# Four moves in a hybrid attention encoder: the rotary exchange on ScalarE, later scores, the first x tiles of chunk two, and w_out's casts behind V's copy

## The chip, the cores and the metric

The kernel runs on one core of a Trainium2 chip. A core has TensorE (matmuls, with a separate load of the weights), VectorE, ScalarE, GpSimd, and SyncE, which here issues nearly all DMAs. The metric is the time of one execution on the device in microseconds (us); less is better.

## The reference

One layer of an encoder with two groups of attention heads, applied to a prompt of 1024 tokens and to a sample of 256 tokens, each with 16 learned meta tokens in front. All is float32.

```python
u = rms_norm(h, norm_w) @ w_in                     # 2048 -> 6656
qa, ka, va, za, qb, kb, vb, zb = split(u)          # 8 q, 2 k, 2 v, 8 gate heads of 128; then 4 x 8 heads
qa, ka = rope(rms_norm(qa)), rope(rms_norm(ka))
ya = softmax(qa @ ka.T / sqrt(128)) @ va * silu(za)          # 8 global heads, 4 to one k and v
qb, kb = rms_norm(qb), rms_norm(kb)
yb = softmax(window(qb @ kb.T) / sqrt(128) + bias) @ vb * silu(zb)   # window of 8 x 16, and the meta tokens
y = h + concat(ya, yb) @ w_out                     # 2048 -> 2048
```

The rotary embedding (rope) acts on the two halves of a head's 128 features apart, one for the row and one for the column: in each half, `_rotate` takes x1*c - x2*s and x1*s + x2*c of two quarters x1 and x2 of 32 features.

## The kernel before

A float32 product is made of three matmuls of fp32r: each operand is split into a high part, a cast on ScalarE (L65), and a low part, a subtraction on VectorE (L66). `split` records both; hi*hi, hi*lo and lo*hi are L219 to L221 in the projection, L368 to L370 in the scores, L409 to L411 in the values and L1038 to L1040 in the output projection. TensorE gets its tiles through this pair, and the names say which: wh and wl for w_in, x for the activations, ph and pl for probabilities, q for queries, yh and yl for the attention's output, wm for w_out.

The tokens are projected in two chunks. Chunk one holds 512 tokens (16 meta, 256 sample, 240 prompt), with the features on the 128 partitions. Chunk two holds the other 784 tokens of the prompt, as a block of 512 and one of 272. A strip is 128 output columns of w_in, one head of q, k, v or the gate z, over 16 tiles of 128 input features. There are 52 strips per chunk, for some of which w_in is read from a copy in DRAM in the second chunk. The result of a strip lies in a bank of PSUM (pool pp) and is evacuated by a function of its kind:

- `qk_evac` (L249) squares it on ScalarE (ms, L252), sums over partitions on GpSimd (m2, L254), and for a rotary strip also copies it times the norm's gain to t (L258), makes ts, in which neighbouring groups of 32 partitions are exchanged, by four DMAs (L261), and forms t*c + ts*s on VectorE (L263 to L265; L263 and L264 in place). `rsqrt` (L72 to L77) gives the factor of the norm, and L268 the finished q or k. Rotary strips are the 8 q and 2 k strips of the global heads: 10 evacuations in chunk one, 20 in chunk two (512 and 272).
- `v_rows` (L278) scales v by the token's norm on VectorE into vt (L280), which TensorE transposes; in chunk two `rows_out` (L521) copies the transposed rows on ScalarE from a bank of the pool tp to vl (L533, and L538 for a last piece of fewer than 128 rows) and stores them. The first product of the output projection takes that same bank, so it waits for these copies.
- `z_evac` (L290) makes the gate.

Attention is generators that are put between strips. `run_due` (L234) is called at places, two per strip; `put(n, f)` (L246) sets a part to run n places on. In chunk one `later` (L710) puts the scores and softmax of a head at the first number of `PARTS`, its values at the second, after the place at which its q strip was made. A softmax takes its maximum over partitions on GpSimd (ma, L319), subtracts it on VectorE (L388), applies the exponential and casts ph on ScalarE, and sums on GpSimd (tot, L337), with VectorE's L346 behind. The last sample head of chunk one runs its attention (`attend_sample`, L415: Sm at L425, S at L429) while chunk two begins. The x tiles of chunk two are loaded, multiplied by the norm's gain and split by `load_all_x` (L148): L162 on ScalarE, L163 on VectorE, for a 512 and a 272 piece of each of 16 tiles kt.

The output projection (`outproj`, L1077) uses seven products in the manner of Strassen; `w_operand` (L1015) splits a tile of w_out (ww into wm) and `y_operand` (L980) one of the attention's output (yl into yh and yl). Its first 16 casts of w_out and its first two of y stand where chunk two's last strips and the last local head end.

A scheduler orders the instructions of each engine from a simulated timeline and the dependencies; a dependency without a semaphore (`NoSync`) can be added by hand to set the order of two instructions on one engine.

Of the kernel before, what the change touches and what calls it, by code (L numbers as in the profile page):

```python
# [25 lines left out]
M3 = 3 * NMETA  # L26
# [18 lines left out]
WTYPE = (0, 1, 1, 2)  # L45
FILL = 1
LATE = 48
PARTS = 2, 6
WCH = 4
LAG = 6  # L50
TH = (NP + NS) // 2
# [1 line left out]
FB = 512  # L53
FH = DM // 2
QA, KA, VA, ZA, QB_, KB, VB, ZB = 0, 8, 10, 12, 20, 28, 36, 44
AGAIN = {KA, VA, ZA} | {a + h for a in (QB_, KB, VB, ZB) for h in range(4, 8)}


class Kern:
# [3 lines left out]
    def split(self, hi, lo, full):  # L63
        nc = self.nc
        self.hi = nc.scalar.copy(hi, full).ins  # L65
        return nc.vector.tensor_tensor(out=lo, in0=full, in1=hi.bitcast(F32), op=ALU.subtract).ins  # L66

    def rsqrt(self, ms, n):

# [78 lines left out]
    def load_all_x(self):  # L148


        nc, self.xload = self.nc, {}
        for kt in range(KT):
            w = self.nw[:, kt:kt + 1]
            self.xs[kt] = []
            ta = self.x.tile([P, 2, NB], F32R, tag="xa", name="x", align_bytes=ALIGN)
            tb = self.xb.tile([P, NX], F32R, tag="xb", name="xb", align_bytes=ALIGN)
            o = 0
            for h, l in ((ta[:, 0], ta[:, 1]), (tb[:, :NT2], tb[:, NX - NT2:])):
                r, n = l.bitcast(F32), l.shape[1]
                with self.tc.issue_after(self.early):  # L160
                    self.xload.setdefault(kt, nc.sync.dma_start(r, self.x2d[kt][:, o:o + n]).ins)
                nc.scalar.activation(h, r, AF.Copy, scale=w)  # L162
                nc.vector.scalar_tensor_tensor(out=l, in0=r, scalar=w, in1=h.bitcast(F32), op0=ALU.mult, op1=ALU.subtract)  # L163
                self.xs[kt].append((h, l))
                o += n
        self.tc.add_manual_dep(self.qstore, self.xload[KT // 2].name, mybir.DependencyInfo(
            mybir.DependencyClass.NoSync, mybir.DependencyReason.DATA), reason="x first")
        self.behind = [None] + [self.xload[c] for c in range(WCH - 1, KT, WCH)]
        for d, c in self.consts:
            with self.tc.issue_after(self.xload[KT - 1]):  # L170
                nc.sync.dma_start(d, c)
# [77 lines left out]
    def qk_evac(self, ps, o, n, wc, rope, segs, full=None):  # L249
        nc = self.nc  # L250
        ms = self.ev.tile([P, n], F32, tag="ev", name="ms")
        nc.scalar.activation(ms[:], ps[:, :n], AF.Square, scale=P ** -0.5)  # L252
        m2 = self.ev.tile([P, n], F32, tag="ev", name="m2")
        nc.gpsimd.partition_all_reduce(m2[:], ms[:], P, RED.add)  # L254
        nc.vector.tensor_tensor(out=m2[:], in0=m2[:], in1=self.eb[:, o:o + n], op=ALU.add)
        if rope is not None:
            t = self.ev.tile([P, n], F32, tag="ev", name="t")
            nc.scalar.activation(t[:], ps[:, :n], AF.Copy, scale=wc)  # L258
            ts = self.ev.tile([P, n], F32, tag="ev", name="ts")
            for i in range(4):  # L260
                nc.sync.dma_start(ts[32 * i:32 * i + 32], t[32 * (i ^ 1):32 * (i ^ 1) + 32])  # L261
            c, s = rope
            nc.vector.tensor_tensor(out=t[:], in0=t[:], in1=c, op=ALU.mult)  # L263
            nc.vector.tensor_tensor(out=ts[:], in0=ts[:], in1=s, op=ALU.mult)  # L264
            nc.vector.tensor_tensor(out=t[:], in0=t[:], in1=ts[:], op=ALU.add)  # L265
        r = self.rsqrt(m2[:], n)
        if rope is not None:
            nc.vector.tensor_tensor(out=r[:], in0=t[:], in1=r[:], op=ALU.mult)  # L268
        else:
            d = r[:] if full is None else full  # L270
            nc.vector.scalar_tensor_tensor(out=d, in0=ps[:, :n], scalar=wc, in1=r[:], op0=ALU.mult, op1=ALU.mult)
        for a, m, hi, lo in segs:
            if lo is None:
                nc.sync.dma_start(hi, r[:, a:a + m])
            else:
                self.split(hi, lo, r[:, a:a + m])

    def v_rows(self, ps, o, n):  # L278
        vt = self.ev.tile([P, n], F32, tag="ev", name="vt")
        self.nc.vector.tensor_tensor(out=vt[:], in0=ps[:, :n], in1=self.rb[:, o:o + n], op=ALU.mult)  # L280
        return vt

    def v_turn(self, vt, offs, m=P):
# [131 lines left out]
    def attend_sample(self, q, zs, k, km, vals, vmeta, tab, ydst):  # L415

        nc = self.nc
        ps = self.sp.tile([P, 2, QB], F32, tag="sp", name="sp")
        ps = ps[:].rearrange("p a b -> p (a b)")
        for i in range(2):  # L420
            nc.tensor.matmul(ps[:, HALF * i:HALF * i + HALF], k[:, P * i:P * i + P], q[:, 64 * i:64 * i + HALF], start=True, stop=True)
        pm = self.sp.tile([P, 2, QB], F32, tag="sp", name="sm_ps")
        nc.tensor.matmul(pm[:M3, 0, :], km, q, start=True, stop=True)
        sm = self.sm.tile([M3, QB], F32, tag="Sm", name="Sm")
        nc.scalar.activation(sm[:], pm[:M3, 0, :], AF.Copy, scale=SCALE)  # L425
        s = self.s.tile([P, 2, QB], F32, tag="S", name="S")
        s = s[:].rearrange("p a b -> p (a b)")
        w = 2 * HALF
        nc.vector.scalar_tensor_tensor(out=s[:, :w], in0=ps[:, :w], scalar=SCALE, in1=tab, op0=ALU.mult, op1=ALU.add)  # L429

        def ap(t, off, dims):
            return bass.AP(t.tensor, t.offset + off, [list(t.ap[0])] + dims)

        def gather(name, op):

            m = self.t.tile([P, QB], F32, tag="t", name=name)
            nc.vector.tensor_copy(ap(m[:], 0, [[192, 2], [1, 64]]), ap(s, 0, [[320, 2], [1, 64]]))
            nc.vector.tensor_tensor(out=m[:, 64:192], in0=s[:, 64:192], in1=s[:, 192:320], op=op)
            return m

        ma = self.all_max(gather("m1", ALU.max), sm)
        v = ap(s, 0, [[HALF, 2], [1, HALF]])
        nc.vector.tensor_tensor(out=v, in0=v, in1=ap(ma[:], 0, [[64, 2], [1, HALF]]), op=ALU.subtract)
        nc.scalar.activation(s[:, :w], s[:, :w], AF.Exp)
        pm3 = self.meta_probs(sm, ma, 1.0)
        tot = self.all_sum(gather("a1", ALU.add), sm)
        yield
        po = self.op.tile([P, QB], F32, tag="po", name="po")
        nc.tensor.matmul(po[:], vmeta, pm3[:], start=True, stop=False)
        for i in range(2):  # L450
            nc.tensor.matmul(po[:, 64 * i:64 * i + HALF], vals[:, i, :], s[:, HALF * i:HALF * i + HALF], start=False, stop=i == 1)
        self.put_y(po, tot, zs, ydst)
# [68 lines left out]
    def rows_out(self, vt, n, dst, o):  # L521

        nc = self.nc
        for a in range(0, n, 4 * P):
            offs = range(a, min(n, a + 4 * P), P)
            full = [x for x in offs if x + P <= n]
            t = self.ev.tile([P, 4, P], F32, tag="ev", name="vl")
            tp = self.tp.tile([P, 4, P], F32, tag="tp", name="tp")
            for i, x in enumerate(offs):
                m = min(P, n - x)  # L530
                self.turn_ins(nc.tensor.transpose(tp[:m, i, :], vt[:, x:x + m], self.ident[:]).ins)
            f = len(full)
            nc.scalar.copy(t[:, :f, :], tp[:, :f, :])  # L533
            nc.sync.dma_start(dst[o + a:o + a + P * f].rearrange("(t p) d -> p t d", p=P), t[:, :f, :])
            if f < len(offs):
                m = n - offs[f]
                t = self.ev.tile([m, P], F32, tag="ev", name="vl")
                nc.scalar.copy(t[:], tp[:m, f, :])  # L538
                nc.sync.dma_start(dst[o + n - m:o + n], t[:])
# [67 lines left out]
    def chunk1(self):  # L607
# [2 lines left out]
        self.due, self.late, self.turn, self.behind, self.turned, self.tie = iter(()), [], False, [], [], (1, 0)  # L610
        self.woff, self.second, self.projected, self.sums = 0, False, 0, self.w_sums()
        self.scale2 = [self.one2.tile([P, T2], F32, tag=n, name=n) for n in ("rb2", "eb2")]
        self.xsq = {}
        self.start_chunk(T1)
        vm3s = self.vm3s
        self.vm3s = vm3s + [self.v.tile([P, P], F32R, tag="vmz", name="vm3")]
# [363 lines left out]
    def y_operand(self, p, t, r):  # L980
        nc = self.nc
        if p in (1, 2):
            his, los, full = [], r, [l[:].bitcast(F32) for l in r]
            for l, f in zip(los, full):
                his.append(self.w.tile([P, WCH, P], F32R, tag="wh", name="yh"))
                self.split(his[-1][:], l[:], f)
            return his, los
        if p == 4:
            v = r[0]
# [24 lines left out]

    def w_operand(self, r):  # L1015
        w = self.x.tile([P, 2, FB], F32R, tag="xa", name="wm", align_bytes=ALIGN)
        self.split(w[:, 0, :], w[:, 1, :], r)
        return w

    def x_load(self, p, t, b):  # L1020

# [292 lines left out]
```

## Time and profile before

| | |
|---|---|
| median of 3 runs | 2173.13 us (2171.66 to 2174.37) |
| profiled execution | 2170.17 us |
| its span, first to last instruction | 2168.4 us |
| TensorE busy | 2154.2 us, 99% of the span |
| VectorE, ScalarE, GpSimd busy | 76%, 51%, 24% |
| TensorE's share of the chain that ended last | 92% |
| granted clock of TensorE | 1.000 |

The profile is one execution. A busy row gives an engine's busy time, its share of the span and its number of instructions. A row of the timeline gives the start in us, the duration in us, the engine, the line, the operation, the tiles written and read, their shape and how many alike stand in the row, and in brackets how long the engine had stood idle and what ended that. A row of waits gives the engine, the tile and line that waited, what it waited for, and then the total in us, the number of times and the longest. SPq is the queue in which SyncE issues DMAs. Durations of neighbouring instructions of an engine overlap at their ends.

### The profile page before, as it was taken

How to read it: one execution, taken by the hardware profiler on the slowest of the kernel's cores; microseconds unless marked ns; L12 is line 12 of the kernel's file. 1: busy time of each engine (PE TensorE's matmuls, PEld its weight loads, DVE VectorE, ACT ScalarE, POOL GpSimd, SP SyncE). 2: the span in 40 equal slices, each digit the busy share in tenths (PEclk: the TensorE clock that was granted, in tenths of full speed). 3: DMA queues.
4: the chain of work that ended last, by engine and by line, in shares of the span. 5: the costliest groups of instructions: out<-in, count | busy, mean ns of one | idle time of the engine just before them, and what ended most of it. 6: DMA issues, size and time to landing. Idle time of an engine off the chain costs nothing.

```text
span 2168.4 us, 34088 instructions
## 1 busy us (share of the span) xinstructions
PE 2154.2 (99%) x11745; PEld 1877.5 (87%) x11745; DVE 1644.9 (76%) x2989; ACT 1115.1 (51%) x2291; POOL 522.7 (24%) x250
## 2 busy tenths in 40 slices
PE   9999999999999999999999999999999999999999
PEld 7888878888888999989999999999999988888887
DVE  7787886777874899896798998677787877545763
ACT  6565554555554666665666666444443454232230
POOL 1232331221311234332133324324333312000000
PEclk9999999999999999999999999999999999999999
DMA  8667789988664333334333344654443364662663
GB/s 301 220 206 224 235 301 308 325 286 278 214 195 144 100 115 107 113 114 132 106 110 106 105 124 145 192 162 131 132 133 122 115 201 152 238 226 99 233 223 107
DMA packets 263182, 383.83 MB, mean 177 GB/s; under 512 B 44992, under 2 KB 112992, under 8 KB 263008
## 3 DMA queue, kind: packets, MB, share of 16 engines
q1 hardware_dynamic: 263008, 381.65, 54.1%
q8 instruction: 92, 1.51, 0.3%
q14 instruction: 82, 0.67, 0.1%
HBM read 281.01 MB, written 100.38 MB: 176 GB/s over the span
## 4 chain that ended last, share of the span: by engine, by line
PE 92%; DVE 3%; DMA 2%; ACT 1%; POOL 1%; issue 1%; SPq 0%; DVEq 0%; POOLq 0%; ACTq 0%
PE pp L219 20%; PE pp L221 20%; PE pp L220 20%; PE pq L1038 6%; PE pq L1040 6%; PE pq L1039 6%; PE po L510 2%; PE sp L476 2%; PE po L409 1%; PE sp L369 1%; PE sp L368 1%; PE po L411 1%; PE po L410 1%; PE sp L370 1%; POOL tot L337 1%
## 5 line engine op out<-in xcount | busy, mean ns | idle before, releaser
L219 PE MATMUL pp<-x,wh 128*128 128x512 f32 (+1 forms) x1664 | 654.5, 395 | 1.7 <-ACT x L162 1.1
L221 PE MATMUL pp<-x,wl 128*128 128x512 f32 (+1 forms) x1664 | 647.9, 390 | 1.1 <-DVE wl L66 1.1
L220 PE MATMUL pp<-x,wh 128*128 128x512 f32 (+1 forms) x1664 | 647.8, 390 | 0.0
L221 PEld LDWEIGHTS pp<-x,wl 128*128 128x128 f32 x1664 | 312.7, 188 | 62.7 <-DVE wl L66 2.0
L219 PEld LDWEIGHTS pp<-x,wh 128*128 128x128 f32 x1664 | 312.5, 188 | 59.3 <-ACT wh L65 2.6
L220 PEld LDWEIGHTS pp<-x,wh 128*128 128x128 f32 x1664 | 313.0, 188 | 52.8
L254 POOL PARTITION_ALL_REDUCE m<-ms x78 | 231.6, 2969 | 406.9 <-ACT ms L252 329.5
L66 DVE TENSOR_TENSOR wl<-wr,wh 128x512 fp32r<-128x512 f32 (+2 forms) x287 | 216.8, 758 | 114.6 <-ACT wh L65 102.2
L337 POOL PARTITION_ALL_REDUCE tot<-a x80 | 182.8, 2285 | 463.3 <-DVE a L334 447.1
L65 ACT CAST wh<-wr 128x512 fp32r<-128x512 f32 (+2 forms) x287 | 174.1, 611 | 202.3 <-PE pp L220 182.3
L220 PE MATMUL pp<-xb,wh 128*128 128x272 f32 x832 | 240.3, 289 | 0.0
L221 PE MATMUL pp<-xb,wl 128*128 128x272 f32 x832 | 239.6, 288 | 0.0
L219 PE MATMUL pp<-xb,wh 128*128 128x272 f32 x832 | 239.5, 288 | 0.0
L1038 PE MATMUL pq<-wm,yh 128*128 128x512 f32 x560 | 218.3, 390 | 0.0
L1040 PE MATMUL pq<-wm,yl 128*128 128x512 f32 x560 | 218.2, 390 | 0.0
L1039 PE MATMUL pq<-wm,yh 128*128 128x512 f32 x560 | 218.0, 389 | 0.0
L319 POOL PARTITION_ALL_REDUCE ma<-m x80 | 101.0, 1262 | 382.1 <-DVE m L317 381.6
L219 PEld LDWEIGHTS pp<-xb,wh 128*128 128x128 f32 x832 | 156.5, 188 | 7.6
L220 PEld LDWEIGHTS pp<-xb,wh 128*128 128x128 f32 x832 | 156.5, 188 | 7.4
L221 PEld LDWEIGHTS pp<-xb,wl 128*128 128x128 f32 x832 | 157.4, 189 | 0.3
L1040 PEld LDWEIGHTS pq<-wm,yl 128*128 128x128 f32 x560 | 105.1, 188 | 21.8
L1039 PEld LDWEIGHTS pq<-wm,yh 128*128 128x128 f32 x560 | 105.1, 188 | 21.7
(211 smaller groups left out, 3840.1 us busy)
## 6 DMA issues: line engine op xcount, KB each, us to landing
wr<-in_w_in SPq DMA_DIRECT2D x413, 256.0 KB, 3.4
wld<-wl SPq DMA_DIRECT2D x132, 256.0 KB, 4.2
wl<-wld SPq DMA_DIRECT2D x132, 256.0 KB, 3.1
yr<-yd SPq DMA_DIRECT2D x35, 512.0 KB, 4.8
wq<-in_w_out SPq DMA_DIRECT2D x64, 256.0 KB, 5.3
td<-wq SPq DMA_DIRECT2D x64, 256.0 KB, 4.5
ww<-td SPq DMA_DIRECT2D x64, 256.0 KB, 5.3
ww<-in_w_out SPq DMA_DIRECT2D x48, 256.0 KB, 5.2
```

Of the source, the lines that this page charges most:

```text
L65: self.hi = nc.scalar.copy(hi, full).ins
L66: return nc.vector.tensor_tensor(out=lo, in0=full, in1=hi.bitcast(F32), op=ALU.subtract).ins
L219: nc.tensor.matmul(p[:, :n], wh[:, k, :], xh[:, :n], start=first, stop=False)
L220: nc.tensor.matmul(p[:, :n], wh[:, k, :], xl[:, :n], start=False, stop=False)
L221: self.lastmm = nc.tensor.matmul(p[:, :n], wl[:, k, :], xh[:, :n], start=False, stop=last).ins
L254: nc.gpsimd.partition_all_reduce(m2[:], ms[:], P, RED.add)
L319: nc.gpsimd.partition_all_reduce(ma[:], m1[:], P, RED.max)
L337: nc.gpsimd.partition_all_reduce(tot[:], a1[:], P, RED.add)
L476: nc.tensor.matmul(dst, k[:, o:o + P], qfv[:, a:e, :], start=True, stop=True)
L1038: nc.tensor.matmul(ps, yh, wh, start=k == 0, stop=False)
L1039: nc.tensor.matmul(ps, yh, wl, start=False, stop=False)
L1040: self.lastmm = nc.tensor.matmul(ps, yl, wh, start=False, stop=k == 7).ins
```

## The change

There are four parts.

1. `PARTS` is 3 and 7 in place of 2 and 6: in chunk one the scores and the values of a head are put one place, half a strip, later.
2. In `qk_evac` ts is made by four ScalarE activations of 32 partitions each, which read the strip from PSUM with the gain of the exchanged group as scale, instead of by four DMAs from t.
3. In `load_all_x` the 512 piece of tile kt = 1 is ordered ahead of the last sample head's Sm on ScalarE, and its second half ahead of that head's S on VectorE. (`place_after(i, j)` puts i behind j on their engine.)
4. `WFIRST` = 5: the casts of w_out numbered 5 to 16, and the split of y for the first tile of product 1, are ordered behind the last vt on VectorE, and on ScalarE behind a vl copy: the last but one copy of `rows_out`'s whole rows for the split of y and the casts up to number 8, the last one from number 9 on.

```diff
-PARTS = 2, 6
+PARTS = 3, 7
+WFIRST = 5
 # qk_evac
             for i in range(4):
-                nc.sync.dma_start(ts[32 * i:32 * i + 32], t[32 * (i ^ 1):32 * (i ^ 1) + 32])
+                j = 32 * (i ^ 1)
+                nc.scalar.activation(ts[32 * i:32 * i + 32], ps[j:j + 32, :n], AF.Copy, scale=wc[j:j + 32])
 # load_all_x
-                nc.scalar.activation(h, r, AF.Copy, scale=w)
-                nc.vector.scalar_tensor_tensor(out=l, in0=r, scalar=w, in1=h.bitcast(F32), op0=ALU.mult, op1=ALU.subtract)
+                a = nc.scalar.activation(h, r, AF.Copy, scale=w).ins
+                d = nc.vector.scalar_tensor_tensor(out=l, in0=r, scalar=w, in1=h.bitcast(F32), op0=ALU.mult, op1=ALU.subtract).ins
+                if kt == 1 and o == 0:
+                    self.place_after(self.lastsm, a, "x first")
+                    self.place_after(self.lasts, d, "x first")
 # y_operand, products 1 and 2
-                self.split(his[-1][:], l[:], f)
+                i = self.split(his[-1][:], l[:], f)
+                if (p, t) == (1, 0):
+                    self.behind_v(i)
 # w_operand
-        self.split(w[:, 0, :], w[:, 1, :], r)
+        i = self.split(w[:, 0, :], w[:, 1, :], r)
+        self.wouts += 1
+        if WFIRST <= self.wouts <= 16:
+            self.behind_v(i)
         return w
+
+    def behind_v(self, i):
+        self.place_after(i, self.lastvt, "drain first")
+        self.place_after(self.hi, self.vlcopies[-1 if self.wouts > 8 else -2], "drain first")
+
+    def place_after(self, i, j, why):
+        self.tc.add_manual_dep(i, j.name, mybir.DependencyInfo(
+            mybir.DependencyClass.NoSync, mybir.DependencyReason.DATA), reason=why)
```

`split` keeps its cast in `self.hi` and returns its subtraction; `lastvt`, `lastsm`, `lasts` and `vlcopies` are kept by `v_rows`, `attend_sample` and `rows_out`.

Three places show how the order moves. The first is VectorE in a q strip of a global head of chunk two, where L268 (L277 in the changed kernel) finishes q, and S<-S,ma is the head ahead's subtraction of the maximum. Before:

```order
L76 TENSOR_TENSOR rs_l<-m_8363,rs_l 128x512
L77 SCALAR_TENSOR_TENSOR rs_r_8378<-rs_l,rs_r_8378 128x512
L388 TENSOR_TENSOR S<-S,ma 128x512 x4
L324 TENSOR_TENSOR Sm<-Sm,ma 48x256
L268 TENSOR_TENSOR rs_r_8378<-t,rs_r_8378 128x512
```

And after:

```order
L81 TENSOR_TENSOR rs_l<-m_8363,rs_l 128x512
L82 SCALAR_TENSOR_TENSOR rs_r_8378<-rs_l,rs_r_8378 128x512
L277 TENSOR_TENSOR rs_r_8378<-t,rs_r_8378 128x512
L362 TENSOR_TENSOR y<-po,z 128x256
L397 TENSOR_TENSOR S<-S,ma 128x512 x4
L333 TENSOR_TENSOR Sm<-Sm,ma 48x256
```

The product that finishes q has moved ahead of the four subtractions.

The second is TensorE at the scores of that same q (q_8237): sp is the scores' bank, pp_8908 a strip's 272 columns, po the values of the head ahead. Before, with the strip's matmuls first and the scores 39 rows on:

```order
L219 MATMUL pp_8908<-xb_6746,wh_8971 128x272
L220 MATMUL pp_8908<-xb_6746,wh_8971 128x272
L221 MATMUL pp_8908<-xb_6746,wl_8972 128x272
L219 MATMUL pp_8908<-xb_6754,wh_8971 128x272
...
L410 MATMUL po_7900<-ph_7911,va_7134 128x256
L411 MATMUL po_7900<-pl_7912,va_7133 128x256
L368 MATMUL sp_8411<-q_8237,kf_6811 128x256
```

And after:

```order
L227 MATMUL pp_8908<-xb_6746,wh_8971 128x272
L228 MATMUL pp_8908<-xb_6746,wh_8971 128x272
L229 MATMUL pp_8908<-xb_6746,wl_8972 128x272
L377 MATMUL sp_8411<-q_8237,kf_6811 128x256
L377 MATMUL sp_8420<-q_8237,kf_6811 128x256
L227 MATMUL pp_8908<-xb_6754,wh_8971 128x272
```

The first matmul of the scores now stands right behind the strip's matmuls with xb_6746.

The third is ScalarE at the start of the output projection, with the casts of w_out (wm<-ww), of y (yh<-yl) and the copies of v's rows (vl<-tp). Before:

```order
L65 CAST wm<-ww 128x512 x5
L65 CAST yh<-yl 128x512
L65 CAST wm<-ww 128x512 x2
L533 COPY vl<-tp 128x512
L65 CAST wm<-ww 128x512 x5
L533 COPY vl<-tp 128x256
L538 COPY vl<-tp 16x128
L65 CAST yh<-yl 128x512
```

And after:

```order
L66 CAST wm<-ww 128x512 x4
L542 COPY vl<-tp 128x512
L66 CAST yh<-yl 128x512
L66 CAST wm<-ww 128x512 x4
L66 CAST yh<-yl 128x512
L542 COPY vl<-tp 128x256
L547 COPY vl<-tp 16x128
L66 CAST wm<-ww 128x512 x4
```

The first copy now stands ahead of the first y cast and of casts 5 to 8, and the last two copies have come behind the second y cast. On VectorE the last vt has moved from behind the low parts of w_out's casts 5 to 7 to right behind number 4. On SyncE the load of that second yl has one load of w_out fewer ahead of it.

More of the change, by code (lines that the diff above doesn't have):

```diff
@@ L279, in v_rows @@
         vt = self.ev.tile([P, n], F32, tag="ev", name="vt")
-        self.nc.vector.tensor_tensor(out=vt[:], in0=ps[:, :n], in1=self.rb[:, o:o + n], op=ALU.mult)
+        self.lastvt = self.nc.vector.tensor_tensor(out=vt[:], in0=ps[:, :n], in1=self.rb[:, o:o + n], op=ALU.mult).ins
         return vt
@@ L424, in attend_sample @@
         sm = self.sm.tile([M3, QB], F32, tag="Sm", name="Sm")
-        nc.scalar.activation(sm[:], pm[:M3, 0, :], AF.Copy, scale=SCALE)
+        self.lastsm = nc.scalar.activation(sm[:], pm[:M3, 0, :], AF.Copy, scale=SCALE).ins
         s = self.s.tile([P, 2, QB], F32, tag="S", name="S")
@@ L428, in attend_sample @@
         w = 2 * HALF
-        nc.vector.scalar_tensor_tensor(out=s[:, :w], in0=ps[:, :w], scalar=SCALE, in1=tab, op0=ALU.mult, op1=ALU.add)
+        self.lasts = nc.vector.scalar_tensor_tensor(out=s[:, :w], in0=ps[:, :w], scalar=SCALE, in1=tab, op0=ALU.mult, op1=ALU.add).ins
         def ap(t, off, dims):
@@ L532, in rows_out @@
             f = len(full)
-            nc.scalar.copy(t[:, :f, :], tp[:, :f, :])
+            self.vlcopies.append(nc.scalar.copy(t[:, :f, :], tp[:, :f, :]).ins)
             nc.sync.dma_start(dst[o + a:o + a + P * f].rearrange("(t p) d -> p t d", p=P), t[:, :f, :])
@@ L612, in chunk1 @@
         self.scale2 = [self.one2.tile([P, T2], F32, tag=n, name=n) for n in ("rb2", "eb2")]
-        self.xsq = {}
+        self.xsq, self.vlcopies, self.wouts = {}, [], 0
         self.start_chunk(T1)
```

## Prediction

> **What bounds the kernel now.** I read the busy times first, then the waits of TensorE, because the first decide whether anything but those waits matters.
>
> ```profile
> PE 2154.2 (99%) x11745; PEld 1877.5 (87%) x11745; DVE 1644.9 (76%) x2989; ACT 1115.1 (51%) x2291; POOL 522.7 (24%) x250
> PE po L409 <- ACT ph L65: 2.6, 3, 1.6
> PE tp L531 <- DVE vt L280: 2.3, 1, 2.3
> PE pp L221 <- DVE wl L66: 1.1, 2, 0.6
> PE tp L287 <- DVE vt L280: 1.1, 1, 1.1
> PE pp L219 <- ACT x L162: 1.1, 1, 1.1
> ```
>
> TensorE is busy for 2154.2 us of a span of 2168.4 us. No matmul is added or taken away, so this change can win only out of the 14.2 us in which TensorE stands still, and the five rows of waits (total, times, longest) hold 8.2 us of that. Everything else is lost or gained as a new wait. The change touches three places where these waits lie, and one long stretch where there is almost none. I take them in the order of time.
>
> **Chunk one, 245 to 283 us: the exchange and the later scores.** The timeline around the first L409 wait, of SyncE, VectorE, ScalarE and TensorE:
>
> ```profile
> 248.44 1.26 SPq L261 DMA_DIRECT2D ts<-t  x2
> 251.61 0.67 DVE L263 TENSOR_TENSOR t<-t,rope 128x496 f32<-128x496 f32 x1 [2.64 <-DMA ts<-t]
> 252.21 0.68 DVE L388 TENSOR_TENSOR S<-S,ma 128x512 f32<-128x512 f32 x1
> 253.77 0.60 ACT L65 CAST ph<-S 128x512 fp32r<-128x512 f32 x1
> 254.42 0.39 PE L409 MATMUL po<-ph,vs 128*128 128x256 f32 x1 [1.64 <-ACT ph L65]
> ```
>
> VectorE stands for 2.64 us at L263, which overwrites t in place and so waits until all four exchange DMAs have read it; the last pair was issued from 248.44 on. Queued behind L263 on VectorE is S minus the maximum (L388), behind that the exponential, the cast ph at 253.77, and TensorE, which waits 1.64 us for it. With the exchange on ScalarE nothing of this is queued on SyncE any more: L388 can run 2.6 us earlier, which is more than the 1.64 us of the wait. So that wait goes.
>
> The other waits of this stretch lie 18 to 30 us later:
>
> ```profile
> 264.04 2.21 DVE L346 TENSOR_TENSOR tot<-tot,r 128x256 f32<-128x256 f32 x1 [2.67 <-ACT r L345]
> 272.56 2.51 DVE L76 TENSOR_TENSOR rs_l<-m,rs_l 128x512 f32<-128x512 f32 x1
> 263.72 3.23 POOL L254 PARTITION_ALL_REDUCE m<-ms  x1 [1.03 <-DMA qd<-qp]
> 272.10 3.40 POOL L254 PARTITION_ALL_REDUCE m<-ms  x1 [5.15 <-ACT ms L252]
> 275.73 0.49 PE L221 MATMUL pp<-x,wl 128*128 128x496 f32 x1 [0.56 <-DVE wl L66]
> 279.32 0.28 PE L287 MATMUL tp<-ident,vt 128*16 128x128 f32 x1 [1.09 <-DVE vt L280]
> ```
>
> This is a pile-up on VectorE. L346 had waited 2.67 us for the reduction of the same head that was late because of the stand at L263; then it took 2.21 us, and L76 took 2.51 us, each beside an all-reduce on GpSimd. What was queued behind them (wl, vt) came late to TensorE. If the head runs some 2.6 us earlier, the queue behind L346 has that much more room, against waits of 0.6, 0.6, 1.1 and the rest of L409. In addition PARTS puts the softmax of the next head half a strip later, out of this crowd. But L76 stays where it is, beside its all-reduce, so I leave one of the L221 waits standing. The L409, L221 and L287 rows of the waits make 2.6 + 1.1 + 1.1 = 4.8 us; less the 0.6 us of one L221 wait, and 0.2 us for what of L409 may lie elsewhere, that is a gain of **4.0 us** (bounds: 1.6 us, if only the first goes, and 4.8 us).
>
> [...]
>
> What the exchange costs on ScalarE:
>
> ```profile
> L258 ACT ACTIVATE t<-pp,nqkw 128x512 f32<-128x512 f32 x12 | 8.2, 685 | 0.0
> L325 ACT ACTIVATE Sm<-Sm 48x256 f32<-48x256 f32 x80 | 32.4, 405 | 0.0
> L345 ACT ACTIVATE r<-r 128x256 f32<-128x256 f32 x80 | 33.0, 413 | 0.7
> L261 SPq DMA_DIRECT2D ts<-t x120: 507/582/627, 45.1 to 1260.9; - x120
>   DVE t L263: 11.6, 8
> ```
>
> 48 partitions cost what 128 do (405 and 413 ns), so each of the four new activations of 32 partitions costs about a whole L258. In a full queue an activation starts before the one ahead has ended; by the rows of the next part a 0.47 us one is followed after 0.37. So about 0.58 us each for 512 columns, 2.3 us for four, and 1.5 us for 272 columns: 10 x 2.3 in chunk one and 10 x 3.8 in chunk two, 61 us more on an engine that is busy half the time. In return 120 issues of 0.58 us leave SyncE's queue, and VectorE's eight stands at L263, 11.6 us in all, lose their cause. In chunk one the weight casts that stand behind t now come 2.3 us later; TensorE's waits for wh are not among the rows, and I cost this at nothing, to 1 us.
>
> **Chunk two's start, 609 us: the first x tiles.**
>
> ```profile
> 609.12 0.38 ACT L425 ACTIVATE Sm<-sm_ps 48x256 f32<-48x256 f32 x1 [5.44 <-PE sm_ps L423]
> 609.40 2.55 ACT L162 ACTIVATE x<-x,nw 128x512 fp32r<-128x512 f32 x4
> 610.16 0.73 PE L219 MATMUL pp<-x,wh 128*128 128x512 f32 x2 [1.08 <-ACT x L162]
> ```
>
> ScalarE stands 5.44 us for the scores of the last sample head and casts x only behind them, and TensorE waits 1.08 us for that cast. Now two casts stand ahead of Sm and fall into the 5.44 us, and VectorE's two halves stand ahead of S. The next two casts are due one tile of matmuls apart and come no later than before. What is late next is the softmax of that head by no more than the 0.4 us of Sm's place, and its values come far later. Gain **1.1 us** (0 to 1.2).
>
> **Chunk two's global heads, 610 to 1280 us.** Little is to be won there, so what matters is whether new waits come.
>
> ```profile
> 920.00:1280.00 360.00, 359.48 (x2321) 328.29 (x2320) 311.59 (x579) 235.96 (x488) 104.05 (x49) 1.00 0.37 115
> 764.95 0.47 ACT L258 ACTIVATE t<-pp,nqkw 128x272 f32<-128x272 f32 x1
> 765.32 0.61 ACT L65 CAST ph<-S 128x512 fp32r<-128x512 f32 x1
> 766.66 0.61 ACT L65 CAST q<-rs_r 128x512 fp32r<-128x512 f32 x1
> 764.95 0.29 PE L221 MATMUL pp<-xb,wl 128*128 128x272 f32 x1
> 770.98 0.29 PE L368 MATMUL sp<-q,kf 128*128 128x256 f32 x1
> ```
>
> In the window row (TensorE, its loads, VectorE, ScalarE, GpSimd) TensorE is short of 0.5 us in 360, VectorE is 87% busy and ScalarE 66%; five strips' exchanges bring it to 255 of 360, 71%. The order on VectorE, shown with the change, finishes q ahead of four subtractions S minus the maximum (0.68 us each in the row of L388) and a small one: some 3 us earlier. TensorE's order uses that: it asks for q behind the matmul of 764.95, at about 765.1; that is 5.9 us ahead of the 770.98 at which it asked before. With q's cast at 766.66, done at 767.3, it would wait 2.2 us (767.3 - 765.1); with the cast 3 us earlier it has 0.8 us to spare. I take **0 us**, with bounds of 1 us of gain (the half microsecond and small delays) and the loss of the first rival.
>
> **The start of the out-projection, 1763 to 1774 us.**
>
> ```profile
> 1768.12 0.58 ACT L533 COPY vl<-tp 128x512 f32<-128x512 f32 x1
> 1772.21 0.36 ACT L533 COPY vl<-tp 128x256 f32<-128x256 f32 x1
> 1772.47 0.25 ACT L538 COPY vl<-tp 16x128 f32<-16x128 f32 x1
> 1773.57 0.62 ACT L65 CAST yh<-yl 128x512 fp32r<-128x512 f32 x1 [0.84 <-DMA yl<-yd]
> 1768.86 0.43 DVE L280 TENSOR_TENSOR vt<-pp,rb 128x272 f32<-128x272 f32 x1
> 1769.44 0.52 PE L531 MATMUL tp<-ident,vt 128*128 128x128 f32 x3 [2.32 <-DVE vt L280]
> 1773.27 0.39 PE L1038 MATMUL pq<-wm,yh 128*128 128x512 f32 x1
> 1763.05 3.70 SPq L1012 DMA_DIRECT2D ww<-in_w_out  x8
> 1767.54 0.50 SPq L976 DMA_DIRECT2D yl<-yd  x1
> ```
>
> TensorE waits 2.32 us (some 2.5 with the weight load) for vt, which stands behind w_out's casts on VectorE. Now vt and the first vl copy stand ahead of casts five and on, and this wait goes: TensorE would reach the first product at 1773.27 - 2.5 = 1770.8. But that product takes the bank of the transposes, so it waits for the last vl copy (L538), and on ScalarE the two last vl copies now stand *behind* the second yh cast, where they stood ahead of it. That cast waits for its load: it ran at 1773.57 after 0.84 us of waiting. One w_out load fewer stands ahead of it on SyncE (0.46 us by 3.70 for eight; about 0.6 us of transfer), so I put it at 1772.9; the two copies then start 0.5 and 0.8 us later, L538 ends near 1774.0, and the product starts there instead of at 1770.8. A wait of 3.2 us for one of 2.5: a loss of **0.8 us**. Bounds: a gain of 2.3 us if the load is in time, a loss of 1.5 us if it lands when it did. The later products have the casts in time, since the load that paces them is the same as before.
>
> **Sum.** -4.0 - 1.1 + 0 + 0.8 = -4.3 us. The profiled execution took 2170.17 us, 3 us below the median of 2173.13, and the difference holds for both: 2165.9 for such an execution, **2168.8 us** for the median.
>
> **Rivals.**
> *ScalarE becomes late in chunk two.* Each of eight q strips puts bursts of 2.3 us between the exponentials and the casts ph, which TensorE awaits, and TensorE asks for q 5.9 us earlier. If half a burst comes through in each strip, 8 x 1.1 = 9 us are lost: +4.7, 2177.8 us. It turns the sign from 0.54 us per strip on. For it: VectorE at 87% leaves little to catch up with, and the row of 0.5 us shows that the margins are thin. Against: ScalarE has a third of its time free there, and the bursts partly stand where it would wait for the all-reduce. Chance 0.20.
> *The pile-up comes back.* VectorE meets the all-reduces as before and chunk one gains 1.6 us: -1.6 - 1.1 + 0.8 = -1.9, 2171.2 us. For it: the long L346 and L76. Against: the room of 2.6 us. Chance 0.12.
> *The load is in time at the out-projection*, and the full 2.3 us is won there: -4.0 - 1.1 - 2.3 = -7.4, 2165.7 us. For it: loads in front become fewer. Against: the 0.84 us. Chance 0.18.
>
> **Numbers.** The forecast has 0.50. About 0.2%, 4.3 us, is what a measurement of this kernel can tell from no change, and the forecast lies on that line: 0.27 of it falls beyond, 0.22 within, 0.01 on the slow side. The third rival adds 0.18 to faster, the second 0.11 to the same and 0.01 to slower, the first 0.15 to slower and 0.05 to the same. Faster 0.45, same 0.38, slower 0.17. The range runs from a little below the third rival, 2164, to near the first, 2177.
>
> **What would show it.** Right: no ts DMA and no wait at L263's successor; no L409 wait near 252; at most one L221 wait near 275; no wait for x at 609; a wait of some 3 us of the first product for the vl copy, behind the yh cast. Wrong: new rows of TensorE waiting for ph, q or wh between 640 and 1280 us that add up to more than 2 us, or no wait at all before the first product.

## The result, and the profile after

The changed kernel takes 2165.39 us (median of 5 runs, 2162.77 to 2166.93) against 2173.13 us before: a ratio of 0.9966, with a 95% interval from 0.9954 to 0.9977. By the medians that is 7.7 us less. The forecast was 2168.8 us, 4.3 us less. The profiled execution took 2166.33 us with a span of 2164.5 us.

Here is TensorE's row of the busy times, its waits (total, times, longest), and two stretches (TensorE, its loads, VectorE, ScalarE and GpSimd, the granted clock, the DMA share, GB/s):

```profile
PE 2154.5 (100%) x11745; PEld 1879.5 (87%) x11745; DVE 1654.7 (76%) x2989; ACT 1187.6 (55%) x2411; POOL 524.2 (24%) x250
PE pq L1056 <- ACT vl L547: 3.8, 1, 3.8
PE pp L227 <- ACT wh L66: 0.6, 1, 0.6
PE tp L296 <- DVE vt L289: 0.3, 1, 0.3
240.00:290.00 50.00, 49.70 (x235) 41.35 (x235) 43.83 (x76) 24.06 (x51) 16.33 (x7) 1.00 0.79 261
920.00:1280.00 360.00, 360.00 (x2329) 329.70 (x2328) 313.41 (x573) 258.86 (x524) 100.62 (x49) 1.00 0.35 109
```

Of the waits for ph, vt, wl and x there is, behind the program's first microseconds, one of 0.3 us left, and in 920 to 1280 us TensorE stands nowhere, with ScalarE at 259 of 360 us, where 255 had been worked out. In place of the wait for vt at the output projection there is one of 3.8 us of the first product, for the vl copy.

In chunk one, VectorE and ScalarE at the values that had waited near 252 us:

```profile
246.10 0.67 DVE L277 TENSOR_TENSOR rs_r<-t,rs_r 128x496 f32<-128x496 f32 x1
246.69 0.68 DVE L397 TENSOR_TENSOR S<-S,ma 128x512 f32<-128x512 f32 x1
249.38 0.61 ACT L66 CAST ph<-S 128x512 fp32r<-128x512 f32 x1
```

S minus the maximum runs right behind the finished q at 246.69, where it had waited until 252.21; the cast ph, at 253.77 before, is done by 250.0.

Here is the last matmul of chunk one, in the profile before and then in the one after:

```profile
607.49 0.38 PE L221 MATMUL pp<-x,wl 128*128 128x496 f32 x1
601.61 0.38 PE L229 MATMUL pp<-x,wl 128*128 128x496 f32 x1
```

TensorE is 5.9 us earlier at the end of chunk one.

The exchange on ScalarE, by shape, and the start of the output projection on SyncE, ScalarE and TensorE:

```profile
L270 ACT ACTIVATE ts<-pp,nqkw 32x512 f32<-32x512 f32 x48 | 32.7, 680 | 0.8
L270 ACT ACTIVATE ts<-pp,nqkw 32x272 f32<-32x272 f32 x40 | 19.2, 480 | 0.6
1759.47 0.33 SPq L985 DMA_DIRECT2D yl<-yd  x1
1754.80 0.58 ACT L542 COPY vl<-tp 128x512 f32<-128x512 f32 x1
1765.29 0.62 ACT L66 CAST yh<-yl 128x512 fp32r<-128x512 f32 x1 [3.53 <-DMA yl<-yd]
1765.81 0.36 ACT L542 COPY vl<-tp 128x256 f32<-128x256 f32 x1
1766.08 0.25 ACT L547 COPY vl<-tp 16x128 f32<-16x128 f32 x1
1762.19 0.39 PE L229 MATMUL pp<-x,wl 128*128 128x512 f32 x1
1766.38 0.79 PE L1056 MATMUL pq<-wm,yh 128*128 128x512 f32 x1 [3.80 <-ACT vl L547]
1766.97 0.63 PE L1057 MATMUL pq<-wm,yh 128*128 128x512 f32 x1
1767.40 0.63 PE L1058 MATMUL pq<-wm,yl 128*128 128x512 f32 x1
```

The first vl copy is early (1754.80). But ScalarE stands 3.53 us for the load of the second yl, the last two vl copies stand behind that cast, and the first product, which could have run behind the matmul of 1762.19, starts at 1766.38. Then something follows that the profile before had shown only in the program's first microseconds (there nine matmuls of 512 columns took 4.02 us, from 1.17 us on): 14 matmuls of 512 columns run at a pitch of 0.43 us (1766.97 to 1767.40, and so on to 1772.5), where the pitch had been 0.23. They cost 2.9 us beyond the stand of 4.0 us (the start at 1766.38 is 4.19 us after the one before, less a pitch of 0.23).

### The profile page after: what moved, and what is told of

The parts are those of the page before. It is cut to its first block, busy times and chain, and to the rows that moved or that the text cites. A ratio compares the mean times of both kernels' runs of the same rounds, so it can differ in the third digit from the quotient of the medians.

```text
span 2164.5 us, 33971 instructions
## 1 busy us (share of the span) xinstructions
PE 2154.5 (100%) x11745; PEld 1879.5 (87%) x11745; DVE 1654.7 (76%) x2989; ACT 1187.6 (55%) x2411; POOL 524.2 (24%) x250
## 4 chain that ended last, share of the span: by engine, by line
PE 98%; DMA 1%; DVE 1%; SPq 0%; ACT 0%; issue 0%; DVEq 0%; ACTq 0%
PE pp L227 22%; PE pp L229 22%; PE pp L228 22%; PE pq L1056 6%; PE pq L1058 6%; PE pq L1057 6%; PE po L519 2%; PE sp L485 2%; PE sp L378 1%; PE sp L379 1%; PE sp L377 1%; PE po L420 1%; PE po L419 1%; PE po L418 1%; PE tp L540 0%; DMA yl<-yd 0%
## 5 line engine op out<-in xcount | busy, mean ns | idle before, releaser
L262 POOL PARTITION_ALL_REDUCE m<-ms x78 | 222.7, 2855 | 356.1 <-ACT ms L260 295.6
L346 POOL PARTITION_ALL_REDUCE tot<-a x80 | 180.6, 2258 | 439.0 <-DVE a L343 408.4
L328 POOL PARTITION_ALL_REDUCE ma<-m x80 | 114.3, 1428 | 452.4 <-DVE m L326 443.7
```

The lines of the kernel that those rows point to most:

```text
L328: nc.gpsimd.partition_all_reduce(ma[:], m1[:], P, RED.max)
L346: nc.gpsimd.partition_all_reduce(tot[:], a1[:], P, RED.add)
```

## The experiments

The theory at this point was: the exchange's DMAs caused chunk one's waits, the x tiles were worth 1.1 us, and part 4 cost time, by the place of two copies and by the slow matmuls that the stand brought. First the last point, and two parts alone.

**The two copies ahead of the second y cast** ("fix"). The 16-row copy is kept as `vltail`, and in `y_operand`:

```diff
                 if (p, t) == (1, 0):
                     self.behind_v(i)
+                    if len(his) == 2:
+                        self.place_after(self.hi, self.vltail, "drain first")
```

> The changed kernel with one more order on ScalarE: the second cast of y (yh, the one that waits for its load) stands behind the last two copies of v's rows. Theory: the changed kernel loses 6.9 us at the first product, 4.0 us of standing for the vl copy behind that cast and 2.9 us in matmuls at a pitch of 0.43 instead of 0.23 us that follow the stand; both are caused by the copy's place. Then the first product starts near 1762.5 us at full pitch, about 1 us is lost where product five waits for yh, and the span falls from 2164.5 to about 2158.6 us, the time to about 2160 us. Rival, the slow matmuls are not caused by the stand but come with the start of the output projection: they stay, and the span is about 2161.5 us. Second rival, the load of y is what TensorE really needs: the wait only moves to product five at full length, 3 us or more.

Measured: 2160.36 us (2160.0 to 2161.3), ratio to before 0.9947 (0.9933 to 0.9961), span 2158.5 us. ScalarE and TensorE of this kernel:

```profile
1761.08 0.37 ACT L542 COPY vl<-tp 128x256 f32<-128x256 f32 x1
1761.35 0.25 ACT L547 COPY vl<-tp 16x128 f32<-16x128 f32 x1
1765.02 0.62 ACT L66 CAST yh<-yl 128x512 fp32r<-128x512 f32 x1 [3.42 <-DMA yl<-yd]
1762.36 0.39 PE L1058 MATMUL pq<-wm,yh 128*128 128x512 f32 x1
1765.69 0.50 PE L1058 MATMUL pq<-wm,yh 128*128 128x512 f32 x1 [0.45 <-ACT yh L66]
```

The copies are done at 1761.6, the first product runs at 1762.36 behind the last matmul of the projection, product five waits 0.45 us for yh, and no matmul there is slow. One profile can't tell more about the slow matmuls, because the runs below show that they sometimes stay away by chance; but the granted clock of a run, averaged over its whole span, tells of them too, and it is 1.000 in all five runs of this kernel, where the changed kernel's five have 0.998, 0.998, 0.999, 0.999 and 1.000. So both losses went with the copies' place. This is the fastest kernel of the study.

**The changed kernel without part 4** (`behind_v` is not called):

> The changed kernel without its part 4 (w_out's casts and the split of y in their old order). Theory: part 4 costs time, because it turns a wait of 2.5 us for vt, after which matmuls kept their pitch of 0.23 us, into 4.0 us of waiting and 2.9 us of slow matmuls. Without it the span is about 4.4 us shorter than the changed kernel's 2164.5, about 2160 us, unless a stand of 2.5 us is sometimes enough for slow matmuls. Rival: part 4 wins its 2.3 us and the slow matmuls come anyway; then this kernel is 2 us or more slower than the changed one.

**The same once more**, for one profile:

> The kernel without part 4 once more, for the matmuls behind its stand of 3.4 us near 1759 us, which kept their pitch of 0.23 us in the first profile. [...] Rival: the length alone decides, with a threshold; then this profile shows none again, but a threshold above 3.4 us contradicts the slow ones after stands of 2.5, 2.6 and 3.3 us in the other two kernels.

Measured: 2164.16 us (2162.37 to 2165.12), ratio 0.9963 (0.9951 to 0.9976), and 2164.26 us. The waits and the stretch 1740 to 1790 us of the first profile, and then of the second:

```profile
PE tp L540 <- ACT wm L66: 3.2, 1, 3.2
1740.00:1790.00 50.00, 46.78 (x256) 40.85 (x255) 36.32 (x74) 27.99 (x57) 7.12 (x4) 1.00 0.65 209
```

```profile
PE tp L540 <- ACT wm L66: 2.4, 1, 2.4
1740.00:1790.00 50.00, 47.58 (x253) 41.34 (x252) 36.44 (x74) 28.06 (x57) 7.12 (x4) 0.97 0.65 209
```

The same program stood 3.2 us at this place and kept a granted clock of 1.00 (the column behind GpSimd's), and in the other execution stood 2.4 us, had eight slow matmuls from 1763 to 1766 us and a mean clock of 0.97. (The rows name a cast of w_out as what ended the stand; vt, which the transposes read, was done on VectorE at 1762.0 and 1761.6, just ahead of TensorE's start.) So length alone does not decide. The time is 1.2 us below the changed kernel's, whose ratio has nearly the same interval: part 4 as it was made is worth nothing, or a little less. The 4.4 us that had been expected came from two single profiles, one with slow matmuls and one without. With the two copies in place part 4 is worth, by two medians that were timed together, 2164.16 - 2160.36 = 3.8 us.

**Before and after, profiled once more:**

> The kernel before, profiled once more. The first profile (2170.2 us, 3 us under the median) showed no slow matmuls behind the stand of 2.5 us near 1767 us. Theory: most executions of it do have slow ones there, up to 3 us of them, which is why the medians of the two kernels lie 7.7 us apart and the two profiles only 3.9 us; a time above 2172 us goes with a row of matmuls at 0.43 us near 1770 us, one near 2170 us without. Rival: the 3 us come from elsewhere, as stalls that are spread over the program; then a time above 2172 us comes without slow matmuls.

> The changed kernel, profiled once more. [...]

Measured: 2173.53 us and 2163.16 us. TensorE and the same stretch of the kernel before:

```profile
1769.95 0.87 PE L531 MATMUL tp<-ident,vt 128*128 128x128 f32 x3 [2.92 <-DVE vt L280]
1772.41 0.63 PE L220 MATMUL pp<-x,wh 128*128 128x512 f32 x1
1740.00:1790.00 50.00, 47.08 (x251) 41.26 (x250) 36.45 (x72) 27.69 (x57) 6.80 (x4) 0.93 0.65 202
```

and of the changed kernel:

```profile
1766.08 0.50 PE L1056 MATMUL pq<-wm,yh 128*128 128x512 f32 x1 [3.12 <-ACT vl L547]
1740.00:1790.00 50.00, 46.88 (x256) 40.77 (x255) 35.59 (x74) 27.96 (x58) 6.64 (x4) 1.00 0.65 209
```

The kernel before has the slow matmuls in this execution, nine of 512 columns and some of 272 from 1770.5 to 1775.8 us, and the changed one has none behind a stand of 3.1 us, at 2163.16 us, where its first profile, with 14, took 2166.33. So the first profile of the kernel before, at 2170.17 us, was one without the slow matmuls that cost some 3 us here. The granted clocks of its runs say how often they come. In the 37 runs of the kernel before that were made beside the experiments, the eight at 1.000, the value of the first profile, took 2170.3 to 2172.1 us; 18 have 0.999; and the eleven at 0.998, the value of this profile, took 2172.5 to 2174.5 us. So most executions have some slow matmuls, and the first profile was one of the fewer without. Of the difference between 3.9 us of span and 7.7 us of medians, 3.0 us are the first profile's distance below its median, and 0.9 us that the profile of the changed kernel, with its 14 slow matmuls, lay above its own.

**PARTS alone** (the kernel before with `PARTS = 3, 7`) **and the exchange alone** (the kernel before with part 2):

> The kernel before with PARTS 3 and 7 alone (scores and values of chunk one half a strip later). Theory: the stand of VectorE at L263 for the exchange DMAs is the cause of chunk one's waits of 5.4 us (240 to 285 us), so they mostly stay, 3 to 5 us of them; the time is within 2 us of before. Rival: the softmax lying in the crowd of the strip's evacuation is the cause; then the waits go with PARTS alone, and the time falls by 4 to 5 us.

> The kernel before with the exchange on ScalarE alone. Theory: the wait of L409 near 252 us goes and of the others at 271 to 282 us at most 1.5 us stays; chunk two's 1.0 us of waits go too; the time falls by 4 to 6 us. Rival: without the later scores the pile-up on VectorE comes back beside the all-reduces; only 1.6 to 2 us are won.

Measured: 2174.46 us, ratio 1.0010 (1.0001 to 1.0018), and 2170.11 us, ratio 0.9990 (0.9981 to 0.9998); the kernel before, timed beside these two, took 2172.30 us. TensorE's four largest waits in 120 to 290 us with PARTS alone, and a row of VectorE:

```profile
PE tp L287 <- DVE vm L66: 2.3, 2, 1.3
PE sp L368 <- ACT qs L65: 1.4, 2, 1.2
PE tp L287 <- DVE vt L280: 0.9, 1, 0.9
PE po L409 <- ACT ph L65: 0.9, 1, 0.9
255.34 0.68 DVE L263 TENSOR_TENSOR t<-t,rope 128x496 f32<-128x496 f32 x1 [2.95 <-DMA ts<-t]
```

VectorE stands at L263 as before (2.95 us), and TensorE's waits, of other tiles for the most part, add up to 6.4 us with two small ones, against 4.6 us before. That they stay is what the theory said; that they grow, and the 2.2 us of loss, is a little more than it said. The exchange alone did less than it said; TensorE's waits in 240 to 290 us, and rows of ScalarE, GpSimd, VectorE and TensorE:

```profile
PE tp L288 <- DVE vt L281: 2.4, 1, 2.4
PE sp L369 <- ACT qs L65: 1.4, 1, 1.4
252.80 0.42 ACT L345 ACTIVATE r<-tot 128x256 f32<-128x256 f32 x1 [3.69 <-POOL tot L338]
271.89 4.49 POOL L338 PARTITION_ALL_REDUCE tot<-a  x1 [4.97 <-DVE a L335]
276.41 0.42 ACT L345 ACTIVATE r<-tot 128x256 f32<-128x256 f32 x1 [2.42 <-POOL tot L338]
277.37 0.67 DVE L76 TENSOR_TENSOR rs_l<-m,rs_l 128x496 f32<-128x496 f32 x1 [2.65 <-ACT rs_l L75]
280.57 0.61 PE L220 MATMUL pp<-x,wh 128*128 128x496 f32 x1
```

The wait of L409 and the stand at L263 are gone, as expected. But ScalarE now runs into r (L345), which waits for the sum of the head's softmax on GpSimd, 3.69 and 2.42 us, and behind r are queued qs, for which the scores wait 1.4 us, and the last step of a strip's norm (L75), for which VectorE stands 2.65 us and TensorE, behind vt, 2.4 us. Slow matmuls follow that second stand too (280.57). So the rival was the nearer one: 2.2 us were won, and with the old places of scores and values the crowd jams at the next engine.

**The mended kernel without part 3, without the exchange, without the later scores.** Each takes that part out of "fix" (the condition of part 3 is false; the DMAs are back; `PARTS = 2, 6`).

> The mended kernel (the one called fix) without part 3, the x tiles ahead of the last sample head's softmax. Theory: TensorE's wait of 1.2 us for x near 609 us comes back and nothing else changes: 1.2 us slower than fix, about 2161.5 us. Rival: the wait is covered by the other parts, and the time is the same as fix within 0.4 us.

> The mended kernel with the exchange by DMAs again. Theory after the two single runs: neither the exchange nor the later scores removes chunk one's waits alone, because with the DMAs VectorE still stands some 3 us at L263 and pushes the later softmax into the next strips; so about the 8 us of waits between 120 and 290 us that PARTS alone showed come back, and 1.0 us in chunk two: 2168 to 2170 us. Rival, the parts simply add: PARTS alone cost about 2 us and the exchange alone won 2 us, so this kernel is only about 2 us slower than fix, 2162.5 us.

> The mended kernel with PARTS 2 and 6 again. Theory: the waits that the exchange alone showed near 252 and 276 us (4.2 us, and 1.5 us of slow matmuls behind the second) come back: 2164 to 2166 us. Rival, the parts simply add: later scores alone cost 2 us, so this kernel is 2 us faster than fix, 2158.5 us.

| kernel | median us | against fix | ratio to before, 95% |
|---|---|---|---|
| fix | 2160.36 | | 0.9947 (0.9933 to 0.9961) |
| without part 3 | 2161.36 | +1.0 | 0.9950 (0.9937 to 0.9962) |
| without the exchange | 2170.48 | +10.1 | 0.9991 (0.9982 to 1.0000) |
| without the later scores | 2165.80 | +5.4 | 0.9968 (0.9956 to 0.9980) |

The last three were timed at another time than "fix"; the kernel before took 2172.30 us beside "fix" and 2172.87 us beside the others, so a difference can be off by about 0.6 us.

One wait of TensorE without part 3, then VectorE's and two of TensorE's waits without the exchange:

```profile
PE pp L227 <- ACT x L167: 1.1, 1, 1.1
```

```profile
DVE t L271 <- DMA ts<-t: 14.8, 13, 2.8
PE tp L295 <- DVE vm L67: 2.3, 2, 1.4
PE sp L376 <- ACT qs L66: 1.4, 2, 1.2
```

The x tiles are worth about 1 us here too. The other two do not add: by the single runs the later scores cost 2.2 us and the exchange wins 2.2 us, by the runs from "fix" they win 5.4 and 10.1 us. The last matmul of chunk one, which runs ahead of all that the other parts change, shows it without the noise of the rest: it starts at 607.5 us in the kernel before, at 610.2 with the later scores alone, at 607.4 with the exchange alone and at 601.6 with both. Each removes one of two jams, VectorE at L263 and ScalarE at r, through which the same strips pass, and only with both gone does TensorE go through chunk one without waiting. That the times do not add is shown by these kernels; that the two stands are the whole reason is read from their rows and was not tested by itself. Without the exchange, TensorE's waits in 120 to 290 us add up to 5.5 us, where about 8 us had been expected.

## Why the prediction was right, and where it was off

**Chunk one.** Forecast 4.0 us with bounds of 1.6 and 4.8; the end of chunk one came 5.9 us earlier. The waits of TensorE in 240 to 290 us fell from 4.6 to 0.3 us; the other 1.6 us stand in no row of waits, and the sum, which was made of such rows, had no term for them. The cause that the prediction gave for the first wait, the stand at L263, is gone. But the step that the first wait goes with the exchange, and that the queue behind L346 then has that much more room, holds only with the later scores, to which it had given a half sentence: alone, the exchange won 2.2 us by the medians, and in its profile nothing at the end of chunk one (607.4 for 607.5 us). The second rival (the pile-up comes back) describes the kernel with the exchange alone, though its jam was on ScalarE behind GpSimd's sum rather than on VectorE. Long VectorE instructions beside all-reduces, on which this rival rested, stayed after the change; two rows of it, each beside an all-reduce of 3.2 to 3.6 us:

```profile
235.46 2.31 DVE L272 TENSOR_TENSOR t<-t,rope 128x496 f32<-128x496 f32 x1
249.51 2.35 DVE L343 TENSOR_TENSOR a<-a,Sm 16x256 f32<-16x256 f32 x1 [0.22 <-ACT Sm L334]
```

But TensorE no longer waits behind them.

**The x tiles.** Forecast 1.1, measured about 1 us, and the wait is gone.

**Chunk two.** Forecast 0, with a bound of 1 us of gain: small delays went, TensorE waited for nothing there after the change, and the stage won 1.3 us. The first rival, ScalarE late, did not happen, and TensorE got q where its order asked for it. The cost on ScalarE was a little higher than worked out: the activations of an exchange did not overlap, so four took 2.7 us for 512 columns (32.7 us for 12) and 1.9 us for 272 (19.2 us for 10), where the prediction had 2.3 and 1.5, and ScalarE's busy time grew by 72.5 us, not 61. In 920 to 1280 us ScalarE was still free for 101 of 360 us.

**The output projection.** The sign, the place and the wait were as forecast: the vl copy behind the second yh, 3.2 us forecast, 3.8 and 3.1 us measured. (3.2 for 2.5 us is a loss of 0.7 us, not the 0.8 of the sum. The 0.6 us of transfer is an estimate: 256 KB at the mean of 402 GB/s of 1773 to 1775 us in the profile before take 0.65 us.) The mis-sized term is what follows a stand. The sum took a stand for its length; in the profiles, stands of 2.3 to 3.8 us cost up to 2.9 us more. So this stage lost 4.5 us in the first profile, where the forecast had 0.8 and at most 1.5: 1.5 us of longer stand and 2.9 us of slow matmuls. The wait of the kernel before could be followed by slow matmuls too, as its second profile shows, so in the medians part 4 as it was made costs only about 1.2 us.

**The total.** Between the two first profiles the stages give -5.9 - 1.1 - 1.3 + 4.5 = -3.8 us, against a forecast of -4.0 - 1.1 + 0 + 0.8 = -4.3 and 3.9 us of span. (The 1.3 is read from the 272-column matmul at 1766.20 us before and 1757.87 us after, 8.3 us earlier, less the 7.0 us that the first matmul of chunk two had gained.) That the sum came out so near was luck: chunk one and chunk two won more than their bounds allowed, and the output projection lost more than its bound. The median, 2165.39 us, is also close to the time of the third rival, 2165.7, and that is chance too: in that rival the load of y is in time, and here ScalarE stood 3.53 us for it. For the medians, the step that failed is the last one of the sum, that the difference holds for the median as for the profiled execution. The profile of before lay 3 us under its median, and this was not a level common to all kernels but a row of slow matmuls that this execution lacked.

## What to carry to other kernels

When engines are near their limits, a stand that is removed shows the next one in the same queue; two edits that alone do little or harm can be worth much together, so take parts out of the best version one at a time as well as putting them in one at a time. When an order is given by hand, look at what waits inside the queue that is ordered: a copy that frees a bank must not stand behind a cast that waits for a load. And if the profiled execution lies off the median of a steady kernel, ask which stall it lacks before carrying its times over; here the granted clock of each run would have told.

## What the runs showed of the hardware

A stand of TensorE can be followed by matmuls at half the rate: 0.43 instead of 0.23 us for 512 columns. The granted clock is 0.50 meanwhile. These are rows of the changed kernel around its stand, four of the first profile and two of the second (TensorE's busy time and count stand behind the length of the stretch, the clock behind GpSimd's):

```profile
1762.35:1765.75 3.40, 0.23 (x2) 0.00 (x0) 0.13 (x1) 0.46 (x1) 0.00 (x0) 1.00 1.10 363
1765.76:1769.17 3.41, 2.79 (x7) 2.21 (x8) 3.23 (x6) 3.41 (x10) 0.00 (x0) 0.50 1.01 358
1769.18:1772.58 3.40, 3.40 (x10) 2.63 (x9) 3.40 (x7) 3.31 (x8) 0.00 (x0) 0.50 0.57 163
1772.60:1776.00 3.40, 3.40 (x20) 3.00 (x19) 1.76 (x4) 1.34 (x3) 0.00 (x0) 1.00 0.70 210
1761.12:1764.53 3.41, 1.84 (x9) 1.18 (x7) 0.96 (x2) 0.62 (x1) 0.00 (x0) 1.00 1.07 372
1764.53:1767.94 3.41, 1.86 (x8) 1.54 (x9) 2.30 (x5) 2.95 (x7) 0.00 (x0) 1.00 1.08 394
```

In the first profile the clock stays at 0.50 for 6.82 us, from 1765.76 to 1772.58 us; in the second it is 1.00 in both rows, with a stand of 3.12 us. These are the ten stands of over 2 us, with the mean clock of the 50 us around each (240 to 290 us for the two near 280 us, 1740 to 1790 us for the others):

| profile | stand, us | mean clock of the 50 us |
|---|---|---|
| changed, first | 3.80 | 0.93 |
| without part 4, first | 3.22 | 1.00 |
| PARTS alone | 3.17 | 0.97 |
| changed, second | 3.12 | 1.00 |
| before, second | 2.92 | 0.93 |
| exchange alone, 279 us | 2.45 | 0.97 |
| fix without later scores, 280 us | 2.45 | 1.00 |
| without part 4, second | 2.42 | 0.97 |
| exchange alone, 1768 us | 2.34 | 0.97 |
| before, first | 2.32 | 1.00 |

A mean of 0.97 is, by estimate from the 0.50 above, 3 us at half the clock (0.03 of 50 us, divided by 0.50), and one of 0.93 is 7 us, near the 6.82 us that were read. The length of a stand alone does not decide whether the clock falls: around stands of 3.22 and 3.12 us the clock stayed at 1.00, and around one of 2.34 us it did not. Nor does the program: each of the three kernels that were profiled twice kept its clock in one execution and lost some of it in the other. What else decides is not shown; no run placed a stand on purpose.
